# Forgetting attention's gate sums as two rows of the logits' second product, with one constant causal mask

## The chip, the cores and the metric

The kernel runs on one core of one Trainium2 chip. The metric is the device time of one execution in microseconds (us). Five engines work side by side, each through its own list of instructions in order: TensorE (PE, matmuls and transposes), VectorE (DVE), ScalarE (ACT), GpSimd (POOL) and SyncE (SP, which issues most DMA transfers). The order on each engine is fixed when the kernel is built; at run time an instruction waits until all that it depends on has finished, and everything behind it on its engine waits with it.

## The reference, cut to what matters

One decoder block on 1024 tokens of width 1024: a normalisation, a projection, eight heads of forgetting attention beside a gated spatial mix, an output projection, and a gated MLP with a short convolution. The change concerns the attention:

```
log_f = log_sigmoid(proj[..., G_END:] + b_forget)     # one gate per token and head
c = cumsum(log_f, axis=1)                             # running sums, (tokens, 8 heads)

logits = einsum('bqhd,bkhd->bhqk', qi, k) * scale     # head size 64, blocks of 128 queries
logits = logits + ci[..., None] - c_k                 # sum at the query minus sum at the key
causal = pi[:, None] >= key_pos[None, :]
logits = where(causal, logits, -inf)
p = softmax(logits)
out = einsum('bhqk,bkhd->bqhd', p, v)
```

The sum at the query, `ci`, is the same for a whole row and falls out of the softmax. The sum at the key, `c_k`, has to be subtracted. (The kernel forms the logits with the opposite sign: the queries carry -1/8, the row extreme is a minimum, the exponential has scale -1.)

## The kernel before, in words

Products run in a 32-bit matmul type of reduced precision. For float32 accuracy a value is kept as a high part (rounded to that type) and a low part (the rest), and a product is made of three: high by high, high by low, low by high. "Splitting" a tile means one rounding copy (`split_w` L154, on ACT where not said otherwise) and one subtraction (L160, on DVE or POOL).

The stages, in order of time: gates and projections of queries and keys (up to about 191 us), values (to about 219 us), attention with the gated half of the output projection between its heads (to about 387 us), then the MLP to the end at 1074.7 us.

*Query and key stage.* `Weights` objects load weight blocks; their method `sums` makes sums of blocks on POOL (L424 to L426), one of them, S2, in a new tile of the buffers named `gg`. `forget` takes two tiles of these buffers, `c` and `r`; `forget_sums` makes the running sums with matmuls and DVE additions, and its `turn` transposes them on PE (L518), writes them, negated, on ACT into a part of `c`, and stores them in DRAM as `ncd`, one row per head. Buffers are few: a later tile of the same name waits for the release of an earlier one.

*Attention.* `head_loads(h)` fetches for head h: `A`, the queries' high and low parts in 64 + 64 partitions; `B`, the keys' high and low parts; `B2`, the keys' parts the other way round; and `ck`, the row `ncd[h]` copied to all 128 partitions. `logits(h, j)` works on query block j (blocks 7 down to 0, n = (j+1) x 128 keys). Per 512 keys it issues A x B (high by high plus low by low, L796) and A x B2 (high by low plus low by high, L797) on PE. Before that a POOL select (L790) writes a big value into the 128 x 128 diagonal block of `ck`, above the diagonal. DVE then adds `ck` to the logits out of PSUM and takes the row's extreme in one operation (L798), and ACT makes the exponential with its row sum (L800). The selects are 64, one per head and block; `sels` collects them. Two PSUM tiles (`pl`) hold logits, so PE's next block waits for the reduce of the block before the last.

`values` turns the exponentials on PE (L813), splits them on ACT and DVE (L814, L815) and multiplies them by V (L832). `row_tail(h)` turns a head's row sums (L738, L739). `pair_half` joins a pair of heads on POOL (L752 to L754).

*The filler.* `sg_out` multiplies the turned gates `sgT` by the output weights `wos`, one product of twelve matmuls (k = 0 to 3, three each, L874 to L876) per call, put between the heads' steps. Its weights come in two halves. The first split is on ACT and POOL, for a filler call that stands behind block 5 of head 0. The second is on ACT and DVE, during head 0's steps. `turn_sg(hf)` turns the gates: PE transposes (L705), ACT copies (L707), DVE subtracts (L708). `wo_load` splits the attention's output weights on POOL.

*What sets the order.* PE's instructions in the attention are chained by `seq` in the order of the program. On the other engines a scheduler sets the order at build time from priorities and dependencies, and `after(tc, x, y)` pins x behind y. Before, POOL's `pair_half` and `wo_load` operations are pinned behind chosen selects. There are no such pins for `split_w` in `sg_out`.

Of the kernel before, what the change touches and what calls it, by code (L numbers as in the profile page):

```python
# [65 lines left out]
def block_kernel(ctx: ExitStack, tc: tile.TileContext, xT, xtok, wuv, wv, wqk, wf, cpk, bfv,  # L66
# [76 lines left out]
    ncd = drm.tile([8, 1024], F32, name="ncd")  # L143
# [312 lines left out]
    def forget():  # L456

        c = sb("gg", [P, 512])
        r = sb("gg", [P, 512], F32R)
        wfa, sel = c[:, 0:128].rearrange("p (a b) -> p a b", b=8), c[0:64, 128:136]  # L460
        bfb, z, e, rows = c[:, 136:144], c[:, 144:208], c[:, 208:272], c[0:64, 272:400]
        tri, ones, lh, ll = r[:, 0:P], r[:, P:2 * P], r[:, 256:320], r[:, 320:384]
# [7 lines left out]
        act.copy(ones, one128)  # L470
        dve.scalar_tensor_tensor(out=tri, in0=maskb, scalar=0.0, in1=ident, op0=ALU.is_gt, op1=ALU.add)
        w = sb(RTAG[rn[0] % 6], [P, 16, 64], F32R)
        rn[0] += 1
        dve.memset(f32(w), 0.0)
        dve.tensor_copy(w[:, :, 0:8], wfa)
        dve.tensor_tensor(out=w[:, :, 32:40], in0=wfa, in1=f32(w[:, :, 0:8]), op=ALU.subtract)
        zr = sb(RTAG[rn[0] % 6], [64, 1024])
        rn[0] += 1
        for hf in range(2):
            ps = sbank()  # L480
            ops = ([("B11", k, k) for k in range(4)] + [("B21", k, 4 + k) for k in range(4)] if hf == 0 else
                   [("B22", k, 8 + k) for k in range(4)] + [("T3", k, 12 + k) for k in range(4)])
            for i, (n, k, wi) in enumerate(ops):
                for s in range(2):
                    pe.matmul(ps[0:64, :], w[:, wi, :], xs(n, s, k), start=(i == 0 and s == 0),
                              stop=(i == 7 and s == 1))
            act.copy(zr[:, hf * 512:hf * 512 + 512], ps[0:64, :])
        return c, r, zr

    def forget_sums(c, r, zr):  # L490
        sel, bfb, z, e, rows = c[0:64, 128:136], c[:, 136:144], c[:, 144:208], c[:, 208:272], c[0:64, 272:400]
# [24 lines left out]

        def turn():
            pe.transpose(ps[0:64, 192:320], z, ident)  # L518
            act.activation(rows, ps[0:64, 192:320], AF.Copy, scale=-1.0)
            sp.dma_start(out=ncd.rearrange("h (t p) -> (h t) p", p=P), in_=rows)  # L520

        return turn

# [204 lines left out]
    loads = [None] * 8  # L728
    exs = []
    rows = [None] * 8  # L730
    sels = [[] for _ in range(8)]

    def row_tail(h):

        p, hh, rs = h // 2, h % 2, rows[h]
        ptr = bank()
        rt = sb("t01", [8, P])
        dve.reciprocal(rs, rs)  # L738
        seq(pe.transpose(ptr[0:8, 0:P], rs, ident))  # L739
        act.copy(rt, ptr[0:8, 0:P])  # L740
        act.dma_start(out=rsd[h], in_=rt)
        sp.dma_start(out=attF[p][hh * 64:hh * 64 + 64, 1, :],
                     in_=rsd[h].rearrange("a b -> (a b)").unsqueeze(0).to_broadcast((64, 1024)))

    def pair_half(p, o):
# [2 lines left out]
            attT[p] = sb("A" if p < 2 else "G", [P, 2, 1024], F32R)  # L748
        f, t = attF[p], attT[p]
        if p < 3:  # L750
            s = sels[2 * p + 3][o.start // 512 * 3:]
            after(tc, pool.tensor_tensor(out=f[:, 0, o], in0=f[:, 0, o], in1=f[:, 1, o], op=ALU.mult), s[0])  # L752
            after(tc, pool.tensor_copy(t[:, 0, o], f[:, 0, o]), s[1])
            after(tc, pool.tensor_tensor(out=t[:, 1, o], in0=f[:, 0, o], in1=f32(t[:, 0, o]), op=ALU.subtract), s[2])  # L754
        else:
            dve.tensor_tensor(out=f[:, 0, o], in0=f[:, 0, o], in1=f[:, 1, o], op=ALU.mult)
            act.copy(t[:, 0, o], f[:, 0, o])
            dve.tensor_tensor(out=t[:, 1, o], in0=f[:, 0, o], in1=f32(t[:, 0, o]), op=ALU.subtract)
# [5 lines left out]
    cks, b2s = sb("x2", [P, 2, 1024]), sb("x2", [P, 2, 1024], F32R)  # L764
# [12 lines left out]

    def logits(h, j):


        i, jj, hh = j // 2, j % 2, h % 2
        A, B, ck, B2 = abs_[h][:, 0, :], abs_[h][:, 1, :], cks[:, hh, :], b2s[:, hh, :]
        w1, w2 = (2 * i + 1) * P, (2 * i + 2) * P
        if jj == 1:
            tp = sb(TTAG[i][hh], [P, w1 + w2])
# [1 line left out]
        t = places[h, i][jj]  # L787
        n = (j + 1) * P
        qs = slice(j * P, (j + 1) * P)
        sels[h].append(pool.affine_select(out=ck[:, qs], in_=ck[:, qs], pattern=[[-1, P]], compare_op=ALU.is_ge,  # L790
                                          fill=BIG, base=0, channel_multiplier=1))
        mn = sml.tile([P, 1], F32, tag="mn", name=nm("mn"))
        ps = psa.tile([P, 1024], F32, tag="L", bufs=2, name=nm("pl"))
        for c in range(0, n, 512):
            e = min(n, c + 512)
            seq(pe.matmul(ps[:, c:e], A[:, qs], B[:, c:e], start=True, stop=False))  # L796
            seq(pe.matmul(ps[:, c:e], A[:, qs], B2[:, c:e], start=False, stop=True))  # L797
        dve.tensor_tensor_reduce(out=t, in0=ps[:, 0:n], in1=ck[:, 0:n], scale=1.0, scalar=lim[:, 0:1],  # L798
                                 op0=ALU.add, op1=ALU.min, accum_out=mn)
        exs.append(act.activation(t, t, AF.Exp, bias=mn, scale=-1.0, accum_out=rows[h][:, j:j + 1]))  # L800

# [43 lines left out]
    def sg_out():  # L845
# [17 lines left out]
        for hf in range(2):  # L863
            o = slice(hf * 512, hf * 512 + 512)
            for tt in range(8):
# [21 lines left out]
    def wo_load(ks):  # L887
        for k in ks:
# [627 lines left out]
```

## Time and profile before

| | |
|---|---|
| median of 3 runs | 1076.82 us (1076.59 to 1077.02) |
| profiled execution | 1076.44 us, of which the span is 1074.7 us |
| granted TensorE clock, mean | 0.998 |
| PE busy | 1054.8 us, 98% of the span |
| DVE busy | 892.9 us, 83% |
| ACT busy | 571.0 us, 53% |
| POOL busy | 237.2 us, 22% |
| SyncE's DMA queue | 159.32 MB, 45.5% of 16 engines' span |

The span runs from the first to the last instruction of one profiled execution; the execution's own time lies around it. Rows of a timeline give the start in us, the duration, the engine, the line, the operation, output<-input, and in brackets the idle time before and what ended it. Rows of the waits give who waited for whom: total us, times, longest. Rows of groups give line, engine, operation, shapes and count, then busy us and mean ns, then the idle time before them and what ended it. A row with "xN" joins N like instructions in a run. Matmuls overlap: one of 512 columns lasts 389 ns, and the next starts 0.23 us after it.

### The profile page before, as it was taken

The numbers are of one execution on the slowest core, as the hardware profiler recorded it, in microseconds if no ns is written. First come the engines' busy times: TensorE is split into PE (matmuls) and PEld (weight loads), VectorE is DVE, ScalarE is ACT, GpSimd is POOL, SyncE is SP. The second block draws the span as 40 slices with busy tenths as digits, with TensorE's granted clock in tenths as the row PEclk, the third lists the DMA queues.
The fourth block names the chain that finished last, engine by engine and source line by source line (L and its number), as shares of the span: only waits on it lengthen the run. The fifth ranks groups of instructions, "written<-read, shape, count | busy, mean of one in ns | idle before, by whom it ended". The sixth has DMA issues, their size and how long they took to land.

```text
span 1074.7 us, 14461 instructions
## 1 busy us (share of the span) xinstructions
PE 1054.8 (98%) x5013; PEld 875.8 (81%) x5013; DVE 892.9 (83%) x1303; ACT 571.0 (53%) x985; POOL 237.2 (22%) x219
## 2 busy tenths in 40 slices
PE   9999999989999899999999999999999999999997
PEld 6888788778888788878888888888888888888886
DVE  5985798777777869999899999989988776898774
ACT  6666644456666845764444444444444444454653
POOL 0002134020223651054333333333322000000000
PEclk9999999999999999999999999999999999999999
DMA  9242257957556335132244523223331899433442
GB/s 338 97 140 97 68 159 213 265 165 215 162 177 225 120 128 185 72 118 97 98 137 161 172 69 127 99 98 99 107 118 46 289 327 319 123 95 97 140 125 96
DMA packets 66297, 160.80 MB, mean 150 GB/s; under 512 B 7976, under 2 KB 8240, under 8 KB 66224
## 3 DMA queue, kind: packets, MB, share of 16 engines
q1 hardware_dynamic: 65792, 159.32, 45.5%
q8 instruction: 39, 0.64, 0.2%
q10 hardware_dynamic: 432, 0.57, 0.1%
q14 instruction: 34, 0.28, 0.1%
HBM read 117.06 MB, written 42.80 MB: 149 GB/s over the span
## 4 chain that ended last, share of the span: by engine, by line
PE 74%; DVE 2%; issue 2%; DMA 2%; ACT 2%; POOL 0%; DVEq 0%; ACTq 0%; POOLq 0%; SPq 0%
PE k L1369 19%; PE qa L1117 11%; PE qc L1117 11%; PE qd L1117 11%; PE qb L1117 5%; PE pb L832 2%; PE pb L813 2%; PE pf L874 1%; PE pf L876 1%; PE pf L875 1%; PE pl L796 1%; PE pl L797 1%; DMA raw<-wos 1%; PE pb L1026 1%; PE pb L1028 1%
## 5 line engine op out<-in xcount | busy, mean ns | idle before, releaser
L1369 PE MATMUL k<-whb,wha 128*128 128x512 f32 x924 | 209.7, 389 | 0.0
L1369 PEld LDWEIGHTS k<-whb,wha 128*128 128x128 f32 x924 | 173.3, 188 | 36.2 <-DVE wha L160 0.2
L1117 PE MATMUL qc<-xT,whb 128*128 128x512 f32 x540 | 129.8, 389 | 0.0
L1117 PE MATMUL qa<-xB,wha 128*128 128x512 f32 x528 | 127.2, 390 | 0.0
L1117 PEld LDWEIGHTS qc<-xT,whb 128*128 128x128 f32 x540 | 101.3, 188 | 21.2 <-ACT whb L154 0.2
L1117 PEld LDWEIGHTS qa<-xB,wha 128*128 128x128 f32 x528 | 98.8, 188 | 20.8 <-DVE wha L160 0.4
L154 ACT CAST wha<-sg 128x512 fp32r<-128x512 f32 x77 | 47.7, 622 | 96.9 <-PE k L1369 86.6
L154 ACT CAST whb<-sg 128x512 fp32r<-128x512 f32 x82 | 50.6, 618 | 85.8 <-PE qc L1117 68.5
L160 DVE TENSOR_TENSOR wha<-sg,wha 128x512 fp32r<-128x512 f32 x77 | 52.8, 688 | 41.0 <-ACT wha L154 40.9
L1117 PE MATMUL qd<-xB,whb 128*128 128x512 f32 x264 | 63.8, 389 | 0.5 <-DVE h L1236 0.5
L1117 PE MATMUL qd<-xT,whb 128*128 128x512 f32 x264 | 63.6, 389 | 0.0
L815 DVE TENSOR_TENSOR pt<-pb,pt 128x512 fp32r<-128x512 f32 (+1 forms) x80 | 50.0, 635 | 14.5 <-ACT pt L814 13.4
L160 DVE TENSOR_TENSOR whb<-sg,whb 128x512 fp32r<-128x512 f32 x82 | 58.3, 711 | 4.4 <-ACT whb L154 4.3
L1117 PE MATMUL qb<-xT,whb 128*128 128x512 f32 x252 | 60.8, 389 | 0.0
L1004 POOL TENSOR_TENSOR sg<-raw 128x512 f32<-128x512 f32 x20 | 30.9, 1546 | 134.2 <-DVE whb L160 76.0
L1117 PEld LDWEIGHTS qd<-xB,whb 128*128 128x128 f32 x264 | 49.5, 188 | 11.2 <-issue 0.9
L1117 PEld LDWEIGHTS qd<-xT,whb 128*128 128x128 f32 x264 | 49.5, 188 | 10.3
L1117 PEld LDWEIGHTS qb<-xT,whb 128*128 128x128 f32 x252 | 47.3, 188 | 9.8
L814 ACT CAST pt<-pb 128x512 fp32r<-128x512 f32 (+1 forms) x80 | 42.5, 539 | 20.6 <-PE pb L813 14.7
L832 PE MATMUL pb<-pt,V 128*128 128x256 f32 x320 | 51.4, 285 | 1.3 <-DVE pt L815 1.2
L790 POOL TENSOR_SCALAR_AFFINE_SELECT x<-x 128x128 f32<-128x128 f32 x64 | 19.9, 312 | 129.7 <-DVE mn L798 77.4
L1007 POOL TENSOR_TENSOR sg<-sg,raw 128x512 f32<-128x512 f32 x20 | 33.3, 1664 | 64.1 <-DVE whb L160 64.1
(396 smaller groups left out, 2305.7 us busy)
## 6 DMA issues: line engine op xcount, KB each, us to landing
raw<-wup SPq DMA_DIRECT2D x44, 512.0 KB, 3.7
sg<-hx SPq DMA_DIRECT2D x77, 256.0 KB, 2.6
hx<-hs SPq DMA_DIRECT2D x44, 256.0 KB, 3.8
hx<-ca SPq DMA_DIRECT2D x35, 256.0 KB, 2.0
xT<-wdn SPq DMA_DIRECT2D x28, 256.0 KB, 4.3
raw<-wqk SPq DMA_DIRECT2D x8, 512.0 KB, 3.6
qd<-G SPq DMA_DIRECT2D x16, 256.0 KB, 3.5
kd<-G SPq DMA_DIRECT2D x16, 256.0 KB, 3.3
```

The costliest lines, as they stand in the source:

```text
L154: act.copy(h, src)
L160: return eng.tensor_tensor(out=l, in0=src, in1=f32(h), op=ALU.subtract)
L790: sels[h].append(pool.affine_select(out=ck[:, qs], in_=ck[:, qs], pattern=[[-1, P]], compare_op=ALU.is_ge, fill=BIG, base=0, channel_multi ...
L796: seq(pe.matmul(ps[:, c:e], A[:, qs], B[:, c:e], start=True, stop=False))
L813: seq(pe.transpose(ptr[:, c:c + P], tj[jj][:, k * P:(k + 1) * P], ident))
L814: act.copy(pt[:, 0, 0:w], ptr[:, 0:w])
L815: dve.tensor_tensor(out=pt[:, 1, 0:w], in0=ptr[:, 0:w], in1=f32(pt[:, 0, 0:w]), op=ALU.subtract)
L832: seq(pe.matmul(po[0][:, oo:oo + n], lhs, pt[:, s, o:o + n], start=(k == 0 and s == 0), stop=(s == 1 and half)))
L1004: pool.tensor_tensor(out=s[0], in0=a21, in1=a22, op=ALU.add)
L1007: pool.tensor_tensor(out=s[3], in0=s[1], in1=a12, op=ALU.add)
L1117: pe.matmul(ps, w[:, wi, ks], xb[:, xi, k, :], start=(first and n == 0), stop=(n == 11), skip_group_check=True)
L1369: pe.matmul(banks[bk + m], xh[:, xi, ms], wh[:, wi, :], start=(first and p_ == 0 and n == 0), stop=(p_ == NP - 1 and n == 2), skip_group_c ...
```

## The change

The running sums enter the logits as a part of the matmul. The first product becomes (query high; query low) by (key high; key high), the second (query high; one; one) by (key low; negated sum high; negated sum low), with 64 + 2 = 66 contraction rows; the low by low term is no longer formed. The rows of ones come from a small tensor `oned` in DRAM, loaded for the first two heads only (the buffers keep them); the sums' high and low rows come from `ncd`, which is stored by `turn` in two transfers. `turn` now writes these rows into `r`, with one more DVE operation for the low part, and no longer uses `c`. The causal mask is one bf16 tile of 1024 columns, zero but for its last 128, made once on POOL; block j reads its last n columns. The 64 selects, the list `sels`, the pins behind them and the broadcast loads of `ck` go. `pair_half` and `wo_load` run unpinned on POOL. The second split of the filler's weights moves its four low parts from DVE to POOL. Line numbers behind the edits grow by up to 12: the first product is L808, the second L809, the reduce L810, the exponential L812, the splits L155 and L161, the gate copies L714, the filler's matmuls L886 to L888.

Bytes of head loads: before 512 (A) + 512 (B) + 512 (ck) + 2 x 256 (B2) = 2048 KB per head; after 512 (A) + 2 x 256 (B) + 256 (query high) + 256 (key low) = 1536 KB and rows of 8 KB.

```diff
         def turn():
             pe.transpose(ps[0:64, 192:320], z, ident)
-            act.activation(rows, ps[0:64, 192:320], AF.Copy, scale=-1.0)
-            sp.dma_start(out=ncd.rearrange("h (t p) -> (h t) p", p=P), in_=rows)
+            rh, rl = r[0:64, 0:P], r[0:64, P:2 * P]
+            act.activation(rh, ps[0:64, 192:320], AF.Copy, scale=-1.0)
+            dve.scalar_tensor_tensor(out=rl, in0=ps[0:64, 192:320], scalar=-1.0, in1=f32(rh),
+                                     op0=ALU.mult, op1=ALU.subtract)
+            for s, t in enumerate((rh, rl)):
+                sp.dma_start(out=ncd[s].rearrange("h (t p) -> (h t) p", p=P), in_=f32(t))
...
+    idr = sb("t01", [P, 1024])
+    msk = idr[:, 0:512].bitcast(BF16)
+    pool.memset(msk[:, 0:1024 - P], 0.0)
+    pool.tensor_copy(msk[:, 1024 - P:1024], maskb)
...
         if p < 3:
-            s = sels[2 * p + 3][o.start // 512 * 3:]
-            after(tc, pool.tensor_tensor(out=f[:, 0, o], in0=f[:, 0, o], in1=f[:, 1, o], op=ALU.mult), s[0])
-            after(tc, pool.tensor_copy(t[:, 0, o], f[:, 0, o]), s[1])
-            after(tc, pool.tensor_tensor(out=t[:, 1, o], in0=f[:, 0, o], in1=f32(t[:, 0, o]), op=ALU.subtract), s[2])
+            pool.tensor_tensor(out=f[:, 0, o], in0=f[:, 0, o], in1=f[:, 1, o], op=ALU.mult)
+            pool.tensor_copy(t[:, 0, o], f[:, 0, o])
+            pool.tensor_tensor(out=t[:, 1, o], in0=f[:, 0, o], in1=f32(t[:, 0, o]), op=ALU.subtract)
...
-        sp.dma_start(out=f32(ab[:, 1, :]), in_=kd[h].rearrange("s d t -> (s d) t"))
-        sp.dma_start(out=cks[:, hh, :], in_=ncd[h:h + 1, :].to_broadcast((P, 1024)))
-        sp.dma_start(out=f32(b2s[0:64, hh, :]), in_=kd[h, 1])
-        loads[h] = sp.dma_start(out=f32(b2s[64:128, hh, :]), in_=kd[h, 0])
+        for s in range(2):
+            sp.dma_start(out=f32(ab[s * 64:s * 64 + 64, 1, :]), in_=kd[h, 0])
+        sp.dma_start(out=f32(a2s[0:64, hh, :]), in_=qd[h, 0])
+        if h < 2:
+            sp.dma_start(out=f32(a2s[64:66, hh, :]), in_=oned)
+        sp.dma_start(out=f32(b2s[64:66, hh, :]), in_=ncd[:, h, :])
+        loads[h] = sp.dma_start(out=f32(b2s[0:64, hh, :]), in_=kd[h, 1])
...
-        sels[h].append(pool.affine_select(out=ck[:, qs], in_=ck[:, qs], pattern=[[-1, P]], compare_op=ALU.is_ge,
-                                          fill=BIG, base=0, channel_multiplier=1))
...
             seq(pe.matmul(ps[:, c:e], A[:, qs], B[:, c:e], start=True, stop=False))
-            seq(pe.matmul(ps[:, c:e], A[:, qs], B2[:, c:e], start=False, stop=True))
-        dve.tensor_tensor_reduce(out=t, in0=ps[:, 0:n], in1=ck[:, 0:n], scale=1.0, scalar=lim[:, 0:1],
+            seq(pe.matmul(ps[:, c:e], A2[:, qs], B2[:, c:e], start=False, stop=True))
+        dve.tensor_tensor_reduce(out=t, in0=ps[:, 0:n], in1=msk[:, 1024 - n:1024], scale=1.0, scalar=lim[:, 0:1],
                                  op0=ALU.add, op1=ALU.min, accum_out=mn)
...
                 if hf == 0 and tt == 7:
-                    whs = split(nxt, "dve")
+                    whs = split(nxt, "pool")
...
-                s = sels[6][4 * k + 2 * hf:] if k < 2 else sels[7][7:] * 2
-                after(tc, pool.tensor_copy(w[hf][:, 0], src), s[0])
-                after(tc, pool.tensor_tensor(out=w[hf][:, 1], in0=src, in1=f32(w[hf][:, 0]), op=ALU.subtract), s[1])
+                pool.tensor_copy(w[hf][:, 0], src)
+                pool.tensor_tensor(out=w[hf][:, 1], in0=src, in1=f32(w[hf][:, 0]), op=ALU.subtract)
```

More of the change, by code (lines that the diff above doesn't have):

```diff
@@ L142, in block_kernel @@
     rbd = drm.tile([8, P], F32, name="rbd")
-    ncd = drm.tile([8, 1024], F32, name="ncd")
+    ncd = drm.tile([2, 8, 1024], F32, name="ncd")
+    oned = drm.tile([2, 1024], F32, name="oned")
     vd = drm.tile([2, P, 2, 512], F32, name="vd")
@@ L460, in forget @@
         wfa, sel = c[:, 0:128].rearrange("p (a b) -> p a b", b=8), c[0:64, 128:136]
-        bfb, z, e, rows = c[:, 136:144], c[:, 144:208], c[:, 208:272], c[0:64, 272:400]
-        tri, ones, lh, ll = r[:, 0:P], r[:, P:2 * P], r[:, 256:320], r[:, 320:384]
+        bfb = c[:, 136:144]
+        tri, ones = r[:, 0:P], r[:, P:2 * P]
         sp.dma_start(out=wfa[:, 0:8, :], in_=wf)
@@ L470, in forget @@
         act.copy(ones, one128)
+        sp.dma_start(out=oned.rearrange("s (t p) -> (s t) p", p=P), in_=f32(ones[0:16, :]))
         dve.scalar_tensor_tensor(out=tri, in0=maskb, scalar=0.0, in1=ident, op0=ALU.is_gt, op1=ALU.add)
@@ L490, in forget_sums @@
     def forget_sums(c, r, zr):
-        sel, bfb, z, e, rows = c[0:64, 128:136], c[:, 136:144], c[:, 144:208], c[:, 208:272], c[0:64, 272:400]
+        sel, bfb, z, e = c[0:64, 128:136], c[:, 136:144], c[:, 144:208], c[:, 208:272]
         tri, ones, lh, ll = r[:, 0:P], r[:, P:2 * P], r[:, 256:320], r[:, 320:384]
@@ L730, in block_kernel @@
     rows = [None] * 8
-    sels = [[] for _ in range(8)]
+    idr = sb("t01", [P, 1024])
+    msk = idr[:, 0:512].bitcast(BF16)
+    pool.memset(msk[:, 0:1024 - P], 0.0)
+    pool.tensor_copy(msk[:, 1024 - P:1024], maskb)
     def row_tail(h):
@@ L736, in row_tail @@
         ptr = bank()
-        rt = sb("t01", [8, P])
+        rt = idr[0:8, 640 + P * hh:640 + P * (hh + 1)]
         dve.reciprocal(rs, rs)
@@ L762, in block_kernel @@
     psa = tc.alloc_tile_pool(name="psb", bufs=4, space=bass.MemoryType.PSUM, reuse_waits="tile")
-    cks, b2s = sb("x2", [P, 2, 1024]), sb("x2", [P, 2, 1024], F32R)
+    a2s, b2s = sb("x2", [P, 2, 1024], F32R), sb("x2", [P, 2, 1024], F32R)
     abs_, places = [None] * 8, {}
@@ L781, in logits @@
         i, jj, hh = j // 2, j % 2, h % 2
-        A, B, ck, B2 = abs_[h][:, 0, :], abs_[h][:, 1, :], cks[:, hh, :], b2s[:, hh, :]
+        A, B, A2, B2 = abs_[h][:, 0, :], abs_[h][:, 1, :], a2s[0:66, hh, :], b2s[0:66, hh, :]
         w1, w2 = (2 * i + 1) * P, (2 * i + 2) * P
```

## The prediction

> **What bounds the kernel now.** I read the page first, then the waits of TensorE by stretch, then the timelines of the engines where TensorE stands still. The page's first part:
>
> ```profile
> PE 1054.8 (98%) x5013; PEld 875.8 (81%) x5013; DVE 892.9 (83%) x1303; ACT 571.0 (53%) x985; POOL 237.2 (22%) x219
> ```
>
> TensorE (PE) is busy 98% of the span. A change that takes no matmul away can only move the few microseconds in which PE waits. The attention stage, which the change edits, lies between 219 and 390 us; its waits are five rows of the waits of PE, and the sixth row is all that PE waits for after 390 us:
>
> ```profile
> PE pb L813 <- DVE pt L815: 2.9, 6, 0.7
> PE pb L739 <- DVE rs L738: 2.6, 2, 1.5
> PE pb L705 <- DVE V L44: 1.9, 1, 1.9
> PE pb L832 <- DVE pt L815: 1.2, 3, 0.6
> PE pl L796 <- DVE mn L798: 1.2, 2, 0.7
> PE qd L1117 <- DVE h L1236: 0.5, 1, 0.5
> ```
>
> Three things are to be seen. All attention waits together are 9.8 us, and none is for GpSimd (POOL). All are for VectorE (DVE). And after 390 us there is only 0.5 us of slack in 684, so whatever the attention stage or an earlier one loses or wins arrives at the end one for one. The price of the change is therefore the change of PE's idle time up to 390 us.
>
> **What is removed: the mask on GpSimd.** The 64 selects and what they cost others:
>
> ```profile
> L790 POOL TENSOR_SCALAR_AFFINE_SELECT x<-x 128x128 f32<-128x128 f32 x64 | 19.9, 312 | 129.7 <-DVE mn L798 77.4
>   POOL x L790: 3.5, 7
> ```
>
> The first row (page, fifth part) is 19.9 us of POOL, an engine 78% idle, so its removal alone is worth nothing. The second row, from the view of line L798, says that DVE's reduce waited for a select 7 times, 3.5 us in all. PE waits for DVE, but these seven waits lie mostly where DVE then catches up before PE needs it. The ends are 0 and 1.5 us (under half of the 3.5); I take 0.3 us, near the lower end, because the attention waits of PE name L798 as releaser in only 1.2 us.
>
> **What is exchanged one for one.** The logits keep two matmuls per 512 columns. The second has 66 contraction rows instead of 128; the reduce reads a bf16 mask instead of an f32 row. Nearest rows, a 64-row weight load and two DVE operations of equal size with bf16 and f32 input:
>
> ```profile
> L496 PEld LDWEIGHTS ps<-gg,whl 64*128 64x128 f32 x16 | 1.9, 187 | 0.8 <-issue 0.4 <-ACT gms L44 0.4
> L44 DVE TENSOR_TENSOR whl<-gg,whl 128x128 fp32r<-128x128 f32 x1 | 0.3, 293 | 0.0
> L44 DVE SCALAR_TENSOR_TENSOR gg<-maskb,ident 128x128 fp32r<-128x128 bf16 x1 | 0.3, 285 | 0.0
> ```
>
> A 64-row load takes 187 ns; loads lie beside the matmuls (81% and 98% in the first row), so a few ns either way would not show. bf16 input takes 285 ns against 293. Both exchanges are costed at nothing; a quicker reduce is a rival below. The smaller head loads, the constant rows' transfer and the second transfer of the sums are on the DMA queue of SyncE, of which PE waits for nothing in the rows above; SyncE's extra issues come long before their readers. Also nothing.
>
> **What is moved, 1: the first split of the output weights (the main term).** Without the pins on the selects, the order in which the changed kernel is built differs. Before, ScalarE (ACT) rounds the four weight halves (L154) as soon as they land, then copies the turned gates (L707), then does the table load and the first exponentials:
>
> ```profile
> 220.94 2.40 ACT L154 CAST whl<-raw 128x512 fp32r<-128x512 f32 x4 [5.88 <-DMA raw<-wos]
> 223.25 2.04 ACT L707 CAST G<-pb 128x512 fp32r<-128x512 f32 x4
> 225.89 1.08 ACT L707 CAST G<-pb 128x512 fp32r<-128x512 f32 x2 [0.60 <-PE pb L705]
> 226.98 1.28 ACT L800 ACT_TABLE_LOAD   x1
> 228.28 1.15 ACT L800 ACTIVATE t<-t,mn 128x1024 f32<-128x1024 f32 x1
> ...
> 229.43 1.03 ACT L800 ACTIVATE t<-t,mn 128x896 f32<-128x896 f32 x1
> ...
> 230.46 1.04 ACT L707 CAST G<-pb 128x512 fp32r<-128x512 f32 x2
> 231.40 0.94 ACT L800 ACTIVATE t<-t,mn 128x768 f32<-128x768 f32 x1
> ```
>
> GpSimd then forms the four low halves. PE turns the gates from 222.15 on:
>
> ```profile
> 222.15 1.53 PE L705 MATMUL pb<-ident,A 128*128 128x128 f32 x12 [1.93 <-DVE V L44]
> ```
>
> PE reaches the fourth weight block (k=3) of its first filler product at 230.45 and ends it at 231.13:
>
> ```profile
> 221.64 5.01 POOL L160 TENSOR_TENSOR whl<-raw,whl 128x512 fp32r<-128x512 f32 x4 [3.80 <-ACT whl L154]
> 230.45 0.39 PE L874 MATMUL pf<-whl,G 128*128 128x512 f32 x1
> ...
> 231.13 0.39 PE L796 MATMUL pl<-x 128*128 128x512 f32 x1
> ```
>
> After, ACT's built order is: four gate copies, three weight halves, one copy, table load, exponentials of blocks 7 and 6, three copies, exponential of block 5, and only then the fourth weight half. In-order, with the durations above: the copies start when the transposes of 222.15 us deliver, about 222.3, and end at 222.3 + 4 x 0.51 = 224.35; three halves of 0.6 to 226.15; a copy to 226.65; the table load to 227.95; the two exponentials (1.15 and 1.03, steps of about 1.15 and 1.0 with their overlap) to 230.1; three copies of 0.52 to 231.65; the exponential of block 5, 0.94, to 232.6; the fourth half, 0.6, to about 233.25. GpSimd's low half takes 5.01 / 4 = 1.25, so it is there at 234.5. PE needs the high half for L874's successor and the low half for the matmul behind it, and is at that place by about 230.4: it stands for about 3 us, does one matmul, and stands about 1 us more. Two matmul steps of 0.23 (0.68 / 3) after 234.5, the filler ends at 235.0 instead of 231.13: **+3.85 us**. The ends are 3.4 (if copies and exponentials run as close together as ACT's best stretch) and 4.3 (one engine handover of 0.1 more at each of four hops). The wait of 0.7 us for L798 that stands behind the next filler doesn't absorb it: it runs from the end of that filler through the reduces of blocks 4 to 2, and these need logits that PE issues only after the late filler.
>
> **What is moved, 2: the sums' tile in the query and key stage.** The negated sums now go as high and low rows into the tile `r`; the tile `c` that held them before is released by the transpose of the gates, and the weight sum of the second projection group (L425) gets c's buffer instead of r's. Rows of before, POOL, PE, then DVE:
>
> ```profile
> 130.24 1.62 POOL L425 TENSOR_TENSOR gg<-raw,raw 128x512 f32<-128x512 f32 x1
> 136.42 0.27 PE L518 MATMUL ps<-ident,gg 128*64 128x128 f32 x1
> 136.45 3.00 PE L402 MATMUL qb<-H,whl 128*128 128x512 f32 x12
> 139.56 0.68 DVE L44 SCALAR_TENSOR_TENSOR G<-G,t 128x512 f32<-128x512 f32 x1
> 140.16 1.21 DVE L44 TENSOR_REDUCE gms<-pt 128x16 f32<-128x1024 f32 x1
> ...
> 144.49 1.72 DVE L44 TENSOR_TENSOR G<-G,gms 128x1024 f32<-128x1024 f32 x1
> ```
>
> The sum, done at 131.9 before, now waits for the transpose at 136.42 and ends at 136.75 + 1.62 = 138.4. The built order puts another product first (12 matmuls from 136.7), then 8 first-term matmuls of three products, 20 x 0.24 = 4.8 us of cover to 141.5, and then needs the low half of that sum. DVE makes it behind the reduce (1.21), two 512-column steps (0.68 each), the new row subtraction (64x128: at most 0.3), a small reciprocal and the 1.72 us product, so at 136.75 + 1.21 + 2 x 0.68 + 0.3 + 0.3 + 1.72 + 0.68 = 142.3 if nothing overlaps; steps of DVE overlap by up to 0.08 each, giving 141.9. PE stands 0.4 to 0.8 us: **+0.6**. Ends: 0 (DVE a little faster, or a later wait takes it up) and 2 (GpSimd's sum also late).
>
> **What is moved, 3: the second split.** Four low halves go from DVE to POOL. Rows: DVE's finish that POOL's pair product needs, the four removed operations (groups by line, 278 to 283 us), PE's wait behind them, POOL's pair product, and PE's matmul with the fourth low half:
>
> ```profile
> 278.00 0.68 DVE L841 TENSOR_TENSOR H<-pb,H 64x512 f32<-64x512 f32 x1
> L160 DVE TENSOR_TENSOR whl<-raw,whl 128x512 fp32r<-128x512 f32 x4 | 2.7, 707 | 0.0
> 283.20 0.55 PE L813 MATMUL pb<-ident,t 128*128 128x128 f32 x3 [0.68 <-DVE pt L815]
> 284.94 1.30 POOL L752 TENSOR_TENSOR H<-H 128x512 f32<-128x512 f32 x1 [0.44 <-DVE H L841]
> 288.09 0.39 PE L875 MATMUL pf<-whl,G 128*128 128x512 f32 x1
> ```
>
> DVE is 2.7 us lighter ahead of the PE wait of 0.68, which should shrink to a remainder set by ACT's copies, about 0.25: **-0.45** (ends -0.7 and 0). On POOL the queue is pair product, low half, cast, low half, subtraction, low half, low half: at most 3 x 1.30 + 4 x 1.25 = 8.9 from 278.7, so 287.6, against 288.09 - 0.45 = 287.65 when PE needs the last one; a cast has one input and should be shorter than 1.30, so something under a microsecond is left. Costed at nothing, with a rival for it.
>
> **Sum.** +3.85 + 0.6 - 0.45 - 0.3 = **+3.7 us**. The profiled execution took 1076.44 us (span 1074.7 and 1.7 around it), so 1080.15; the median of the runs is 1076.82, 0.38 above it, which gives **1080.5**.
>
> **The rivals.**
> *A (faster): the reduce with the bf16 mask is quicker.* DVE holds 7.9 of the 9.8 us of attention waits that don't belong to the values' own stage (all but L705's 1.9). If the reduce were cheaper by a good part of itself, up to 7.9 us would go: 1080.15 - 7.9 + 0.38 = 1072.6. It decides when more than 3.7 + 2.15 = 5.9 of these 7.9 us go. The L815 waits are partly for ACT's copies, and 285 against 293 ns says bf16 buys 3%: unlikely, 0.07. A first split that isn't late after all, with 1.5 us from the POOL waits, gives 1076.8 + 0.6 - 0.45 - 1.5 = 1075.5, no measurable change.
> *B: the clock.* The page's granted clock stays at full in every slice:
>
> ```profile
> PEclk9999999999999999999999999999999999999999
> ```
>
> with PE's longest attention gap 1.9 us. The new gap is 3 us, then 1 more. If the clock halves after it for as long as the stall of 3 to 4 us, PE loses half of that time, and at worst nearly all of it through what waits for it: 1080.5 + 1.5 to 3.5 = 1082.0 to 1084.0. A gap as long is in none of the rows, so 0.12. The Trainium skill's page "TensorE: Matmul & The Clock Gate", section "Part 1: The HAM clock gate", says that one idle window of about 3.4 us, free-running, halves the clock until a busy one has passed; by that rule a 3 us gap with 0.25 us of work in 4 is just at the edge.
> *C: the second split is late.* The same POOL operation that takes 1.25 to 1.30 here took 1.62 at 130 us. At 1.62 for seven operations the last low half comes at 278.7 + 11.3 = 290.0, 2.4 us late: 1080.5 + 2.4 = 1082.9. 0.10. The Trainium skill's "GPSIMD Engine Reference", section "8. Key points", says GpSimd shares its SBUF interfaces with VectorE and is hindered by its instructions with two SBUF inputs; by that rule the lower price holds, as DVE's work at 280 to 288 us reads PSUM.
> *D: the late first split is absorbed or smaller*, because the waits for the rows' DVE work (2.6 us for L738, 4.1 for L815) shrink when DVE runs ahead during the stall: 3.7 - 2 = +1.7, 1078.5. 0.12.
>
> **Chances.** Forecast 0.56, A 0.07, B 0.12, C 0.10, D 0.12, and 0.03 for something better by chance. A measurement of this kernel can tell about 0.2%, 2.15 us. Slower by more than that: forecast, B, C = 0.78; within it, D and a tail = 0.13; faster, A and a tail = 0.09. The range for 8 in 10 runs from D's lower part, 1077.0 (the sum with the low ends 3.4 + 0 - 0.7 - 1.5, and 1 us absorbed), to 1084.0 (B's upper end, C's price inside it); A is left out below it.
>
> **What would show it.** In the profile after: ACT's fourth weight cast at about 232.6, behind an exponential; one POOL L160 low half alone at 233.3; a PE wait of about 3 us for ACT and 1 us for POOL near 231 to 234; PE idle of 0.4 to 0.8 us near 141; the PE wait at 283 shrunk; reduces of unchanged duration. It is wrong if the fourth cast comes with the other three, if the reduce's duration moves by over 5%, or if PE's waits behind 300 us shrink by more than 2 us.

## The result, and the profile after

The changed kernel takes 1086.96 us (median of 5 runs, 1085.63 to 1087.22); the kernel before, run beside it, 1076.94 (5 runs). The ratio is 1.0091, interval 1.0077 to 1.0105: slower by 10.0 us by the medians, where +3.7 was forecast and the range ended at 1084.0. The profiled execution of after took 1086.17 us, its span is 1084.5, its mean granted clock 0.995.

The page of after, the line of busy time and the line of the granted clock in 40 slices:

```profile
PE 1058.9 (98%) x5013; PEld 878.5 (81%) x5013; DVE 891.8 (82%) x1300; ACT 571.2 (53%) x985; POOL 221.4 (20%) x161
...
PEclk9999999989999999999999999999999999999999
```

PE has the same 5013 matmuls, and they lasted 4.1 us longer together: not all of the loss is waiting. The ninth slice of the clock (217 to 244 us) is an 8, the only one. The waits of PE in after, before 219 us (two of three rows):

```profile
...
PE ps L259 <- DVE G L44: 0.7, 1, 0.7
PE qb L403 <- DVE whl L44: 0.5, 1, 0.5
```

and from 219 to 400 us, and behind that:

```profile
PE pb L750 <- DVE rs L749: 2.6, 2, 1.5
PE pf L886 <- ACT whl L155: 2.4, 1, 2.4
PE pf L886 <- DVE pt L827: 2.1, 2, 1.1
PE pb L712 <- DVE V L44: 1.9, 1, 1.9
PE pb L844 <- DVE pt L827: 1.7, 4, 0.6
PE pb L825 <- DVE pt L827: 1.1, 2, 0.5
PE pf L887 <- POOL whl L161: 0.8, 1, 0.8
PE pl L808 <- DVE mn L810: 0.7, 1, 0.7
PE pb L1037 <- DVE H L853: 0.4, 1, 0.4
PE pf L886 <- DVE G L715: 0.4, 1, 0.4
```
```profile
PE qc L1128 <- ACT whb L155: 0.6, 1, 0.6
PE qd L1128 <- DVE h L1247: 0.5, 1, 0.5
```

Four rows are new at the filler (L886, L887). The 2.4 for ACT and the 0.8 for POOL are the late weight half that was forecast. The 0.4 for DVE's subtraction of the gates (L715), a wait right before the same product, and the 2.1 for DVE's `pt`, two waits of 1.05 us before a filler product, were not. The timeline of ACT shows the order that the prediction read from the build, and the fourth half at 232.98 (forecast 232.6) behind an exponential:

```profile
223.47 1.56 ACT L714 CAST G<-pb 128x512 fp32r<-128x512 f32 x3 [2.00 <-PE pb L712]
224.93 1.67 ACT L155 CAST whl<-raw 128x512 fp32r<-128x512 f32 x3
226.55 0.59 ACT L714 CAST G<-pb 128x512 fp32r<-128x512 f32 x1
227.16 1.28 ACT L812 ACT_TABLE_LOAD   x1
...
232.05 0.95 ACT L812 ACTIVATE t<-t,mn 128x768 f32<-128x768 f32 x1
...
232.98 0.61 ACT L155 CAST whl<-raw 128x512 fp32r<-128x512 f32 x1
```

The timeline of PE there:

```profile
233.64 0.51 PE L886 MATMUL pf<-whl,G 128*128 128x512 f32 x1 [2.40 <-ACT whl L155]
234.99 0.80 PE L887 MATMUL pf<-whl,G 128*128 128x512 f32 x1 [0.84 <-POOL whl L161]
235.58 0.63 PE L888 MATMUL pf<-whl,G 128*128 128x512 f32 x1
236.01 0.63 PE L808 MATMUL pl<-x 128*128 128x512 f32 x1
...
241.52 0.40 PE L888 MATMUL pf<-whl,G 128*128 128x512 f32 x1
```

Matmuls of 512 columns last 0.63 us behind the stall and 0.40 again at 241.52. The windows of that stretch, in steps of 3.41 us (columns: window, its length, busy us and number on PE, PEld, DVE, ACT, POOL, granted clock, DMA share, GB/s):

```profile
231.22:234.63 3.41, 0.53 (x2) 0.19 (x1) 1.89 (x3) 2.37 (x5) 0.96 (x1) 1.00 0.00 0
234.63:238.04 3.41, 3.05 (x8) 2.57 (x9) 1.31 (x2) 0.00 (x0) 0.30 (x1) 0.50 0.29 103
238.04:241.46 3.42, 3.42 (x9) 2.65 (x9) 1.03 (x4) 1.70 (x4) 0.00 (x0) 0.50 0.40 128
241.46:244.87 3.41, 2.67 (x14) 2.14 (x13) 1.98 (x7) 0.96 (x3) 0.00 (x0) 1.00 0.20 74
```

The clock was granted at half for 6.83 us, from 234.63 to 241.46. Lining up the same matmuls of the two traces gives how far after lags behind before at each place (a lag that grows is time lost there), and so where the 9.73 us between the two profiled executions arose:

| place (us, before) | lag from, to | part | forecast |
|---|---|---|---|
| to 222.15 | 0 to 0.63 | sums' tile (0.5 seen as a wait at 142) | +0.6 |
| 222.15 to 227.60 | 0.63 to -0.02 | a 0.44 us wait for the first reduce at 227.60 is gone | 0 |
| 228.2 to 230.68 | -0.02 to 4.31 | late fourth half; 0.53 of it is the wait for the gates in front | +3.85 |
| 230.7 to 234.6 | 4.31 to 7.46 | clock at half | rival B |
| 276.83, 319.06 | +0.82, +0.84 | two waits for `pt` before a filler product | none |
| 283 | -0.88, +0.4 | second split on POOL, and a part of the wait at 276.83 given back (see g3) | -0.45 |
| 284 to 359 | -0.44 | several small waits | -0.3 |
| 387, 471 | +0.48, +0.79 | waits for `H` and `whb` | none |

### The profile page after: what moved, and what is told of

Its sections match the earlier page's. It is cut to its first block, busy times and chain, and to the rows that moved or that the text cites. A ratio compares the mean times of both kernels' runs of the same rounds, so it can differ in the third digit from the quotient of the medians.

```text
span 1084.5 us, 14295 instructions
## 1 busy us (share of the span) xinstructions
PE 1058.9 (98%) x5013; PEld 878.5 (81%) x5013; DVE 891.8 (82%) x1300; ACT 571.2 (53%) x985; POOL 221.4 (20%) x161
## 3 DMA queue, kind: packets, MB, share of 16 engines
q1 hardware_dynamic: 64920, 155.25, 44.6%
## 4 chain that ended last, share of the span: by engine, by line
PE 74%; DVE 3%; ACT 3%; issue 2%; POOL 0%; DVEq 0%; ACTq 0%
PE k L1380 19%; PE qa L1128 11%; PE qc L1128 11%; PE qd L1128 11%; PE qb L1128 5%; PE pb L844 2%; PE pb L825 2%; PE ps L259 2%; PE pf L886 1%; PE pf L887 1%; PE pf L888 1%; PE pl L808 1%; PE pl L809 1%; PE pb L1037 1%; PE pb L1039 1%
## 5 line engine op out<-in xcount | busy, mean ns | idle before, releaser
L155 ACT CAST wha<-sg 128x512 fp32r<-128x512 f32 x77 | 47.8, 622 | 96.8 <-PE k L1380 85.7
L155 ACT CAST whb<-sg 128x512 fp32r<-128x512 f32 x82 | 50.6, 618 | 86.4 <-PE qc L1128 66.3
L161 DVE TENSOR_TENSOR wha<-sg,wha 128x512 fp32r<-128x512 f32 x77 | 52.8, 687 | 39.6 <-ACT wha L155 39.5
L827 DVE TENSOR_TENSOR pt<-pb,pt 128x512 fp32r<-128x512 f32 (+1 forms) x80 | 50.0, 635 | 15.7 <-ACT pt L826 14.7
L161 DVE TENSOR_TENSOR whb<-sg,whb 128x512 fp32r<-128x512 f32 x82 | 58.2, 710 | 4.4 <-ACT whb L155 4.3
L844 PEld LDWEIGHTS pb<-pt,V 128*128 128x128 f32 x320 | 44.3, 190 | 4.1 <-PE pb L825 1.4
```

Source lines behind the costliest of these rows:

```text
L155: act.copy(h, src)
L161: return eng.tensor_tensor(out=l, in0=src, in1=f32(h), op=ALU.subtract)
L827: dve.tensor_tensor(out=pt[:, 1, 0:w], in0=ptr[:, 0:w], in1=f32(pt[:, 0, 0:w]), op=ALU.subtract)
L844: seq(pe.matmul(po[0][:, oo:oo + n], lhs, pt[:, s, o:o + n], start=(k == 0 and s == 0), stop=(s == 1 and half)))
```

## The experiments

The theory at this point: the late half costs 4 us, the clock behind it 3, and two places where another engine's order changed cost 0.8 each. The rivals: the late half alone costs it all through later waits; or the rows and the bf16 mask have a price of their own. Zero matmuls in the diffs below are added work without effect on the output. In kernels with more code the line numbers are a few higher.

**e1: the halves first again** (after; `his` are the four casts, `sgc` and `sgl` the gates' copies and subtractions, `exs` exponentials, `reds` reduces).

```diff
+        for x, y in ((sgc[0], his[-1]), (exs[0], sgc[5]), (exs[1], exs[0]), (reds[0], sgl[3]), (reds[1], sgl[4])):
+            after(tc, x, y)
```


> The changed kernel with pins that restore the earlier order around the first split alone: all four weight halves ahead of the gate copies on ScalarE, the first two reduces behind the gates' low parts on VectorE. Theory (late fourth half, and the slow TensorE clock that its stall brings): both go, 3.7 + 3.15 us off 1087.0, so about 1080.1, no half clock at 235 to 241 us. Rival 1 (the clock falls for another reason, such as the two short products or the gate stage as a whole): only 3.7 us off, 1083.3, with the half clock still there. Rival 2 (what follows takes it up): 1085 or more.

Measured: 1079.6 us (10 runs, 1077.03 to 1080.86), ratio 1.0021 (1.0011 to 1.003). Five pins take away 7.4 of the 10.0 us by the medians, and the waits of the filler for ACT and POOL are gone. So most of the loss is the place of these copies. But the profile shows a clock at half again, now behind the old wait for V of 1.93 us, which before has too:

```profile
219.81:223.22 3.41, 1.48 (x13) 1.16 (x12) 2.68 (x7) 2.82 (x6) 2.31 (x2) 1.00 0.32 121
223.22:226.63 3.41, 3.41 (x14) 2.92 (x12) 2.73 (x5) 1.70 (x3) 2.67 (x3) 0.50 0.25 82
```

Four of the ten runs, this one among them, have a mean clock of 0.996 and took 1079.57 to 1080.86 us; the five at 0.998 or 0.999 took 1077.03 to 1079.7.

**e2: the stall filled with matmuls** (after).

```diff
+                    if hf == 0 and tt == 0 and k == 3:
+                        for _ in range(9):
+                            seq(pe.matmul(ps, msk[:, 0:P], msk[:, 0:512], start=False, stop=False))
```


> The changed kernel with nine more matmuls of zeros (added to the same sum, 512 columns each, about 2.0 us) in the first filler product between its third and fourth weight block, where TensorE stands 2.4 us for ScalarE. The fourth half comes no earlier, so the stall stays but TensorE is busy in it. Theory (the standing time halves the clock): full clock throughout, 3.15 us off, about 1083.8. Rival (the clock falls for another reason, or the loss after 235 us is not the clock but late exponentials): still half clock, 1087.

Measured: 1084.61 us (4 runs, 1084.22 to 1085.88), ratio 1.0076 (1.0061 to 1.0091). It is 2.35 us under after, but tells little: the stall was filled only in part, its rest of 1.0 and 0.8 us still brought the clock down for 3.41 us at 236.4, and this execution had another such stretch behind the wait for V. g1 below repeats it better.

**e3: the late half in the kernel before**, everything else as it was.

```diff
         whs = split(load(0), "pool")
+        after(tc, his[-1], exs[2])
```


> The kernel before with one pin: the fourth weight half behind the exponential of block 5 of head 0. Nothing else of the change is in it. Theory: a stall of about 3.3 us at 231 to 234 us as in the changed kernel and the half clock after it, +3.5 + 3.1, so 1083.5. Rival 1 (late half without clock): 1080.4. Rival 2 (the late half is harmless on its own): 1077.

Measured: 1083.84 us (4 runs, 1081.57 to 1084.71), ratio 1.007 (1.0053 to 1.0087), +7.2 us by the medians. One pin in the old kernel brings back as much as the five of e1 take away. Its PE timeline and its windows:

```profile
232.33 0.49 PE L877 MATMUL pf<-whl,G 128*128 128x512 f32 x1 [3.08 <-ACT whl L156]
...
233.68 0.61 PE L878 MATMUL pf<-whl,G 128*128 128x512 f32 x1 [0.85 <-POOL whl L162]
```
```profile
230.50:233.91 3.41, 0.73 (x2) 0.42 (x3) 1.18 (x2) 1.77 (x4) 1.26 (x1) 1.00 0.00 0
233.91:237.32 3.41, 3.41 (x10) 2.74 (x10) 1.58 (x3) 0.36 (x1) 0.29 (x1) 0.50 0.43 154
```

The same two waits and the same fall of the clock, without any row of the change. The profiled execution had only one 3.41 us stretch at half, where after had two, and was the quickest of the four.

**e4: the sums' rows back in the tile `c`** (after).

```diff
-            rh, rl = r[0:64, 0:P], r[0:64, P:2 * P]
+            rh, rl = (c[0:64, n:n + P].bitcast(F32R) for n in (208, 336))
```


> The changed kernel with the two rows of the sums written into a free part of the tile c instead of r, so that the projection's weight sum gets its earlier buffer. Theory (the buffer makes the weight sum late): the 0.46 us wait at 142 us goes and the start of the attention is 0.6 us earlier, 1086.4; what follows is as in the changed kernel. Rival (other DVE work around it sets the wait): no change, 1087.0.

Measured: 1084.62 us (4 runs, 1082.48 to 1087.12), ratio 1.0075 (1.0056 to 1.0094). The intervals of e4 and after overlap, so the total decides nothing; the trace does. POOL's sum is back at 129.85 and the wait at 142 is gone, but the one at 194 (0.70 in after) has grown by what was won:

```profile
194.79 3.74 PE L259 MATMUL ps<-wy,x 128*128 128x512 f32 x15 [1.63 <-DVE G L44]
```

At 227.6 the lag behind before is -0.14 us here and -0.02 in after. In these traces the tile's term was a real wait, and worth 0.1 us.

**g1: the clock alone.** After, with its own orders of copies pinned so that they stay, and zero matmuls where PE stood (f1 was the first form, with 16 more meant for the wait for V; these ran behind that wait instead, and cost 1.9 us of their own).

```diff
+                    for _ in range(20 if first else 0):
+                        seq(pe.matmul(ps[:, 0:256], zt[:, 0:P], zt, start=False, stop=False))
                     seq(pe.matmul(ps, sgT[k][:, 0, ts_], w[:, 0, :], start=(k == 0), stop=False))
+                    for _ in range(7 if first else 0):
+                        seq(pe.matmul(ps[:, 0:256], zt[:, 0:P], zt, start=False, stop=False))
```


> The changed kernel with zero matmuls of 256 columns in all three places where TensorE stands: 16 in the 1.9 us stall at 221 us (overwritten by the transposes behind them), 20 and 7 in the 2.4 and 0.8 us stalls of the first filler product (added zeros). The orders of the other engines are pinned to those of the changed kernel, so the late fourth half stays. Theory (a stretch of about 3.4 us in which TensorE stands for half or more brings 3.4 or 6.8 us of half clock): full clock in every run, 1086.2 - 3.15 = 1083.0, little spread. Rival (half clock has another cause): 1086 to 1087, half clock between 220 and 242 us as before.

> The changed kernel with zero matmuls of 256 columns only inside the first filler product: 20 where TensorE stands for the fourth weight half, 7 where it stands for its low half. The orders of the other engines are pinned to those of the changed kernel. Theory (the standing time in the filler halves the clock): no half clock at 235 to 241 us in any run, 1086.2 - 3.15 = 1083.0. Rival (half clock has another cause): half clock there, 1086 to 1087. f1 did not tell this cleanly, since its zero matmuls for the 221 us stall ran behind that stall and added about 1.9 us.

Measured: f1 1084.13 us (5 runs, 1083.35 to 1085.2), ratio 1.0064 (1.0051 to 1.0078), mean clock 0.998 to 0.999 in each run. g1 1083.73 (5 runs, 1082.88 to 1083.82) beside 1076.77 of before, ratio 1.0062 (1.0049 to 1.0074). The windows of g1, the first of them with PE kept busy where it stood in after:

```profile
231.00:234.60 3.60, 3.42 (x27) 2.54 (x25) 1.89 (x3) 3.52 (x8) 0.00 (x1) 1.00 0.03 13
234.70:241.40 6.70, 6.35 (x32) 4.91 (x32) 3.02 (x7) 1.63 (x4) 1.17 (x1) 1.00 0.30 109
```

The late half is just as late, and PE has done nothing more that counts; but the clock stays whole in this execution, and 3.2 us of after's median are gone. Lined up with the matmuls of after, g1 gains 2.98 us between 235 and 241.5 us, where the table has 3.15 for the clock. The price of the clock is thus shown by itself.

**f3: the change with the orders of ACT and DVE put back.** e1's pins, e4's rows, and in heads 2 and 4 the exponential of block 4 behind the copy of `pt` (POOL stays as in after: the second split is there, and `pair_half` runs unpinned):

```diff
+        if s == 3 and h in (1, 3):
+            after(tc, exs[8 * h + 11], ptc[STEPS[n + 1][0]])
```

The third pin answers the two waits of 1.05 us. The timelines of ACT at the first of them, before and then after:

```profile
274.79 0.94 ACT L800 ACTIVATE t<-t,mn 128x768 f32<-128x768 f32 x1 [1.69 <-DVE mn L798]
275.72 0.46 ACT L814 CAST pt<-pb 128x384 fp32r<-128x384 f32 x1
276.08 0.83 ACT L800 ACTIVATE t<-t,mn 128x640 f32<-128x640 f32 x1
```
```profile
282.18 0.94 ACT L812 ACTIVATE t<-t,mn 128x768 f32<-128x768 f32 x1 [1.69 <-DVE mn L810]
283.11 0.81 ACT L812 ACTIVATE t<-t,mn 128x640 f32<-128x640 f32 x1
283.92 0.83 ACT L826 CAST pt<-pb 128x384 fp32r<-128x384 f32 x2
```

The exponential has overtaken the copy. DVE's subtraction (L827) comes behind this copy, and PE's filler product waits for the subtraction: the copy comes one exponential, 0.81 us, later.

> The changed kernel with every order that differed in the attention put back: first split as in e1, rows of the sums in c as in e4, and the exponential of block 4 of heads 2 and 4 behind the copy of turned probabilities that it overtook on ScalarE (two places, 0.85 us of filler wait each by the drift against before at 277 and 319 us). Theory (nothing of the change itself costs time, only the orders it leads to): 1.7 below e1, median about 1077.5, 1076.9 or less by the fastest runs. Rival (the overtaking is harmless): as e1, 1079.6.

Measured: 1076.0 us (11 runs, 1074.7 to 1078.14), ratio 0.9997 (0.9988 to 1.0006). With these orders of before, the change as a whole costs nothing and brings nothing that can be told.

**g3: the overtaking alone, in before** (two pins, the copy of `pt` behind the exponential and the copy to `H` behind that).

```diff
+        if s == 3 and h in (1, 3):
+            after(tc, ptc[STEPS[n + 1][0]], exs[8 * h + 11])
...
+        if s == 3 and h in (1, 3):
+            after(tc, hcs[-1], ptc[STEPS[n + 1][1]])
```


> The kernel before with the order of the changed kernel at two places only: on ScalarE the exponential of block 4 of heads 2 and 4 ahead of the copy of turned probabilities. Theory (each overtaking makes a filler product wait 0.8 us for its bank, and nothing gives it back): +1.6, 1078.0, with two waits of about 1 us of the filler matmul for the probabilities' low part. Rival (the selects' waits on VectorE hide it, or it is given back at the next head): 1076.4.

Measured: 1078.84 us (11 runs, 1077.32 to 1079.98), ratio 1.0016 (1.0007 to 1.0024), +1.7 us by the ratio and 2.1 by the medians. Two rows of its waits of PE, the first with two of 1.4 where after has two of 1.05:

```profile
PE pf L876 <- DVE pt L817: 2.8, 2, 1.4
PE pb L815 <- DVE pt L817: 2.1, 5, 0.7
```

The second row (L813 in before) had six waits and 2.9 us there: the one of 0.68 at 283 us is gone, although the second split is still on DVE. The lag behind before grows by 1.28 at the first place, falls by 0.81 at 283, and grows by 1.28 at the second; 1.43 us are left at the end. So the overtaking costs time, but a part of the first wait is given back at the next wait for DVE, against the expectation. In after the same can lie in the -0.88 at 283, so the table's 1.66 for the two waits and its -0.48 at 283 can't be priced apart.

**g4: the second split back on DVE, with f3's orders.**

```diff
-                    whs = split(nxt, "pool")
+                    whs = split(nxt, "dve")
```


> f3 with the second split's low halves on VectorE as in the kernel before. Theory (the move of the four low halves to GpSimd is worth the 0.45 us of the wait at 283 us): +0.45 against f3, 1076.5, and the 0.7 us wait back. Rival (GpSimd is late with them, so the move costs as much as it gives): same as f3 or 0.5 below.

Measured: 1078.73 us (11 runs, 1076.58 to 1080.05), ratio 1.0013 (1.0003 to 1.0022): 1.7 us more than f3 by the ratios, 2.7 by the medians. The timeline of PE in g4, and the windows around it:

```profile
284.17 0.55 PE L830 MATMUL pb<-ident,t 128*128 128x128 f32 x3 [1.63 <-DVE pt L832]
```
```profile
282.13:285.54 3.41, 1.73 (x12) 1.25 (x11) 3.38 (x7) 1.56 (x3) 0.23 (x1) 1.00 0.75 229
285.54:288.95 3.41, 3.41 (x11) 2.83 (x10) 3.03 (x8) 1.50 (x6) 2.90 (x3) 0.50 1.01 285
```

The move to GpSimd is worth more here than the 0.45 that was forecast: without it DVE makes PE wait 1.63 us, where before had 0.68, and this execution then has the clock at half. The work on DVE is the same four low halves in the same order as in before, but they take 1061 ns each, where before has 707. A row of g4's groups from 278 to 284 us, and POOL's timeline there:

```profile
L163 DVE TENSOR_TENSOR whl<-raw,whl 128x512 fp32r<-128x512 f32 x4 | 4.1, 1061 | 0.0
```
```profile
278.36 1.30 POOL L765 TENSOR_TENSOR H<-H 128x512 f32<-128x512 f32 x1 [53.83 <-DVE H L858]
279.72 0.95 POOL L766 CAST A<-H 128x512 fp32r<-128x512 f32 x1
280.75 1.60 POOL L767 TENSOR_TENSOR A<-H,A 128x512 fp32r<-128x512 f32 x1
```

The pair product (L765), which stands behind a select at 284.94 in before, here runs beside the low halves, without its pins, and both engines are slower: POOL's cast takes 0.95 us and its subtraction 1.60, where they take 0.61 and 1.28 at 287 us in the same trace; of DVE's four, the one that starts after POOL has ended takes 0.68 us, the other three 1.09 to 1.31. That the one slows the other is read from these rows; no run moves the pair product alone. If it is so, the move of the split mends what the removal of these pins costs. Without the move the change, with the other orders put back, is slower than before by 0.03% to 0.22%.

**f2, f4 and g2: the wait for V filled.** f2 is before, f4 is f3, each with 16 zero matmuls for the wait for V; g2 is f3 with 7 in a free PSUM tile.

```diff
+            for _ in range(16 if hf == 0 and c == 1 else 0):
+                seq(pe.matmul(ps[:, 0:256], zt[:, 0:P], zt, start=True, stop=True))
```
```diff
+                for _ in range(7):
+                    seq(pe.matmul(pz[:, 0:256], zt[:, 0:P], zt, start=True, stop=True))
```


> The kernel before with 16 zero matmuls of 256 columns in its only long stall, 1.9 us at 220 us. Theory (that stall halves the clock for 3.4 us in those runs in which it falls whole into one stretch of the clock's own measure, about (3.4 - 1.9) / 3.4 = 4 in 10): the slower runs go, all near 1075.8, median 0.8 below the kernel before, no half clock in the profile at 222 us. Rival (the spread of the runs has another source): same median and spread as before, 1076.7.

> f3 with the 16 zero matmuls of f2 in the stall at 220 us. Theory: no half clock in the attention, 1075.3 in all runs, 0.4 below f2 by the lighter VectorE at 283 us. Rival 1 (the change has a cost of its own beside the orders): 1 us or more above f2. Rival 2 (the change has a gain of its own, from the waits for GpSimd): 1 us or more below f2.

> f3 with 7 zero matmuls of 256 columns into a sum tile of the logits, which is free 0.7 us before the bank that TensorE waits for at 221 us. This splits the standing time of 1.9 us into 1.2 us and busy time. Theory (the slow ones among the runs of f3 come from half clock after that stall): no half clock at 222 to 226 us, all runs near 1075.3, median 0.7 below f3 and 1.1 below the kernel before. Rival (the spread has another source, or the zero matmuls delay the transposes): 1076 or more, spread as in f3.

Measured: f2 1078.03 us (11 runs), ratio 1.0013 (1.0004 to 1.0022); f4 1077.99 (11 runs), 1.001 (1.0001 to 1.0019); g2 1076.5 (11 runs, 1075.47 to 1079.04), 1.0001 (0.9992 to 1.001). f2 and f4 missed their aim: their matmuls needed the PSUM tile that the wait is about, ran behind it, and cost 1.9 us. They agree with each other, as f3 and before do. In g2 the wait was 1.4 us, and no stretch at half clock is in its profile, yet it is no quicker than f3, and its runs lie as far apart. The mean clocks of the single runs say more: in f3 the six at 0.998 or 0.999 took 1074.7 to 1076.0 us and the five at 0.996 or 0.997 took 1076.94 to 1078.14, while all eleven of g2 have 0.998 or 0.999. So a lower clock goes with the longer runs of f3, and something else spreads those of g2. Where the clock fell in f3's longer runs no trace shows, and what else spreads the runs is not settled.

## Why the prediction was wrong

*The main term* was right in its mechanism: the fourth half came at 232.98 (forecast 232.6), its low half alone on POOL at 233.67 (233.3), PE waited 2.40 and 0.84 us (3 and 1):

```profile
233.67 1.27 POOL L161 TENSOR_TENSOR whl<-raw,whl 128x512 fp32r<-128x512 f32 x1 [4.28 <-ACT whl L155]
```

It cost 4.33 us, the upper end of 3.4 to 4.3; 0.53 of that is the wait for the gates' subtraction ahead of the product, which the sum doesn't have. With the sums' tile the prediction had 4.45 for both, and at this point of the trace after lags by 4.31. That the two together are only 0.14 us off is luck: the late half cost 0.48 more than forecast, and the +0.6 of the tile was given up by 227.6 (its lower end, 0).

*The step that failed first is that the sum prices the stall of 3 and 1 us at full clock, and leaves the half clock to rival B.* The clock did halve, and it cost 3.15 us, in the rival's range of 1.5 to 3.5; forecast and B together, 1080.5 + 3.15 = 1083.65, would have been inside the range. The prediction gave it 0.12 because "a gap as long is in none of the rows", and took its own 3 us for a stall just at the edge. The Trainium skill's "TensorE: Matmul & The Clock Gate", "Part 1: The HAM clock gate", speaks of one idle window of about 3.4 us. The length agrees (every stretch at half clock in the attention lasted 3.41 us or, in after and e4, twice that), but the runs show that PE need not be idle through it: a window with 1.48 us of work was enough in e1, one of 1.73 in g4. With PE at 0.53 us in its window, after was not at the edge.

*The step that failed second is "What is removed: the mask on GpSimd".* It asked only what DVE gains where a reduce no longer waits for a select, not what then runs ahead of what; of ACT the built order was compared around the first split alone. The selects had also held DVE's reduce back:

```profile
275.15 0.89 DVE L798 CUSTOM_DVE_ANT_0 t<-pl,x,lim 128x640 f32<-128x640 f32 x1 [0.40 <-POOL x L790]
```

That is one of the seven waits whose end the prediction booked at -0.3. In after the reduce has no such wait and the exponential stands ahead of the copy of `pt`; the two places, for which the sum had nothing, cost 1.66 us, a part of which may be given back at 283; what the seven waits brought is at most the 0.44 net by which the lag fell from 284 to 359 us. That the select's wait is why the built order was different is inferred from the two timelines; that the order costs time is shown by g3, 1.7 us by the ratio with waits longer than after's.

*Right, but less cleanly than it looks:* the second split. The lag falls by 0.48 at its place in after, against -0.45; but g3 shows that a wait given back falls into the same place, and f3, which has the split and not that wait, gains 0.34 there. The sum also left out what g4 points to, that the unpinned pair product slows the low halves where they stay on DVE. Rival C did not come: POOL's low halves took 1.27 to 1.29 us, and no row of PE's waits after 235 us names POOL. The reduce did not change, as the groups of its line show (before 875/1080/1275), so rival A had nothing to work with, nor did the 66-row weight load (190 ns in the median):

```profile
L810 DVE CUSTOM_DVE_ANT_0 t<-pl,t,lim x16: 873/1082/1277, 225.9 to 364.0; 128x1024 f32<-128x1024 f32 x4, 128x896 f32<-128x896 f32 x4, 128x768 f32<-128x768 f32 x4, 128x640 f32<-128x640 f32 x4
```

*Left open:* the two waits at 387 and 471 us, 1.27 us together. The first (0.4) is also in f3, with no loss in its total, and in e3, the kernel before with one pin, so it needs none of the rows of the change. The second is not in the profiles of e4 and g1, whose order at the filler is after's, so it doesn't come with every execution of it.

The ledger: 4.3 late half + 3.15 clock + 1.66 overtaking - 0.48 at 283 us - 0.44 + 1.27 open = 9.5 of 9.73. The 15.8 us of work taken from GpSimd, and the smaller head loads (SyncE's queue: 159.32 MB to 155.25), brought nothing that can be told: f3 is at 0.9997.

## What to carry to other kernels

An edit that removes pins or work changes the built order of every engine: compare all of them, through the whole stage, ahead of pricing what was removed, because here the order alone was worth about 10 us and the removed work nothing that could be told. When a stall leaves TensorE less than about half busy in a stretch of 3.4 us, count with a clock at half behind it as a real chance, 1.7 us more for each 3.41 us window; the three windows here with 0.53 to 0.73 us of work (after, e4, e3) all brought it. When a removal leaves another engine free to run ahead, ask which short copy for the bounding engine it can now overtake, and pin that one; and ask which operations of two engines now run at the same time, as GpSimd's pair product and the low halves in g4.

## What the runs showed of the hardware

The granted clock changed only at steps of 3.41 us: the windows that came down began at 223.2 (e1), 222.8 and 236.4 (e2), 233.9 (e3), 234.6 (after), 285.5 us (g4); between the two falls of e2 lie 13.65 us, four such steps. Each fall brought one or two windows at half clock. It came back behind a window in which PE was busy throughout (3.41 of 3.41 in e1, e3, g4), and in after not behind the one with 3.05 of 3.41, the one that held the end of the wait for POOL, nor in e4 behind one with 2.96: there 0.36 and 0.45 us of idle went with a second window. The border by work done was not sharp: 1.48 us of PE in a window were followed by half clock in e1, 1.50 in e4 (220.76 to 224.17) and 1.61 in after (220.97 to 224.39) were not, 1.73 in g4 were, 2.15 in before were not. The same wait for V of 1.93 us was followed by a half clock in the profiles of e1 and e2 and not in those of before, after, e3, e4 and f3, so it costs about 1.7 us (half of 3.41) or nothing; what decides beside the work in the window is not shown.
